# Low parts of X without GpSimd at the two ends of a sequence half, and X loaded once there

## The chip, the cores and the metric

The kernel runs on one core of a Trainium2 chip. A core has five engines that each work through their own instruction queue in order: TensorE (PE: matrix products, with PEld for its weight loads), VectorE (DVE), ScalarE (ACT), GpSimd (POOL) and SyncE (SP, which here only issues DMAs). The metric is the time of one execution on the device in microseconds (us); the median of several runs is given.

## The reference

One decoder block on x (2048 x 1024, fp32) with two token mixers. What the change touches is the first line, the combined input projection; the rest is shown cut:

```python
proj = x @ w_in + b_in                      # (2048, 1024) @ (1024, 9216)
q, k, v, g_attn, u_lru, g_lru, gate_logits = split(proj)
attn = dilated_band_attention(rope(q), rope(k), v) * silu(g_attn)     # three head groups
h    = rg_lru(causal_depthwise_conv(u_lru)) * silu(g_lru)
merged = sigmoid(gA) * (attn @ w_attn_proj) + sigmoid(gB) * (h @ w_lru_proj)
out  = layer_norm(alpha * x + merged @ w_out + b_out)
```

log a in the RG-LRU is -8 r softplus(-lambda), so a softplus of a 1024-vector is needed before the first gate.

## The kernel before

**Numbers.** All matrix products keep fp32 accuracy with operands split into a high and a low part (fp32r): the high part is a rounded copy made by ACT, the low part is the difference (source minus high part), made by DVE or POOL. A product of one 128 x 512 output tile over 512 of the contraction is four K tiles times three matmuls: (w high, x high), (w high, x low), (w low, x high), 12 in all.

**The projection (phase A).** Weight columns are taken in pairs of 128-column blocks: 36 pairs, and for each of the two halves of the sequence one *position* per pair, 72 positions. One position is a 2 x 2 block product: weights A11, A12, A21, A22 (two column blocks, two halves of the contraction) against x blocks B11, B21 (first 512 columns of the half) and B12, B22 (second 512). The first position of each half (s = 0 and s = 36) is computed plainly in eight *ticks*; all others by seven products (Strassen-Winograd, table `MID`, or `EDGE` for the last position of a half): A11·B11, A12·B21, S4·B22, A22·T4, S1·T1, S2·T2, S3·T3. S1 to S4 are sums of weight blocks, T1 to T4 combinations of the x blocks, made once per half. A tick is the time of one product, 12 matmuls; `base[s]` is the tick at which position s starts (0, 8, 15, ..., 253 for s = 36, 261 for s = 37).

**The order.** `manual_schedule` runs each engine in the order of the program text. The loop over ticks writes the product of the tick, then the functions that `at(t, ...)` has put down for it, then the running *chains* (generators that ask for time on engines and are continued when the tick has some left), and then the evacuation of the product's PSUM bank. The product tiles use four PSUM banks in turn (`q`), so the fifth product waits until the first one's bank has been read. An engine that waits holds all that stands behind it.

**Weights.** `load_w` loads a block; for the first half `added` forms S1 and S3 by a DMA that accumulates onto the loaded tile, issued from POOL's queue, `sums` forms S2 and S4 on DVE. `prep_w` makes the high part on ACT and the low part alternately on POOL and DVE; the low parts are kept in DRAM (`wl_scr`) and loaded again for the second half.

**X at the beginning (ticks 0 to 9) and at the change of half (from E0 = base[36] - 7 on).** Each x block has four K tiles of 128 x 512 (256 KB). `load_raw` loads one from DRAM through SP's queue, `hi_lo` makes its two parts; `one_block` does so for a B block, K tiles alternating between DVE and POOL for the low part, and gives the raw tile back. The combinations need the raw data again: `comb_loads` loads all four blocks a second time (tiles `xcB..`), `comb` makes of one K tile T1, T2, T3 and a first step of T4 on DVE, with the copies on ACT and the low parts of T1 and T3 on POOL, and `fourth` makes the parts of T4. T4 shares its place in SBUF with B12, so its copies wait until the plain position is through with B12.

**Around it.** `evacuate` reads a product's bank: product 1 into a copy e by ACT, the others into sums (u, v) and results on DVE; `result` hands a finished tile to a chain (bias, tanh or silu, rotary), and for the merge gates `mg_chain` stores it to `mg_scr` by a DMA on SP. Six small constant operations on DVE and the 25 of softplus stand at the kernel's head and at tick 10, each as one block.

In the traces a name such as xB stands for xB11, xB12, ...; hA and hS are high parts of weights, l low parts, S weight sums, wA and wS raw weights. `hi_lo` is L217 to L221, `tt` L232, so most DVE and POOL operations carry L232 and the parts of X L220 (copy) and L221 (low part); the products are L614.

## Time and profile before

| | |
|---|---|
| time, median of 3 runs | 2311.54 us (2310.54 to 2316.93) |
| profiled execution: time / span | 2308.68 us / 2306.9 us |
| mean granted TensorE clock | 0.983 of full speed |
| DMA: bytes, mean rate | 523.92 MB, 227 GB/s |

The span is the profiled stretch of the program; the time of the same execution lies 1.8 us above it. A page of the profile gives busy time by engine, groups of instructions by source line with the idle time of the engine just before them and what ended it, and DMA issues; the trace behind it can be asked for a timeline of one engine, or for windows with the busy time of every engine in each.

### The profile page before, as it was taken

How to read it: one execution, taken by the hardware profiler on the slowest of the kernel's cores; microseconds unless marked ns; L12 is line 12 of the kernel's file. 1: busy time of each engine (PE TensorE's matmuls, PEld its weight loads, DVE VectorE, ACT ScalarE, POOL GpSimd, SP SyncE). 2: the span in 40 equal slices, each digit the busy share in tenths (PEclk: the TensorE clock that was granted, in tenths of full speed). 3: DMA queues.
4: the chain of work that ended last, by engine and by line, in shares of the span. 5: the costliest groups of instructions: out<-in, count | busy, mean ns of one | idle time of the engine just before them, and what ended most of it. 6: DMA issues, size and time to landing. Idle time of an engine off the chain costs nothing.

```text
span 2306.9 us, 34335 instructions
## 1 busy us (share of the span) xinstructions
PE 2224.7 (96%) x11008; PEld 1871.6 (81%) x11008; DVE 1753.8 (76%) x3192; ACT 1090.9 (47%) x1977; POOL 940.0 (41%) x684
## 2 busy tenths in 40 slices
PE   6999999999999799999999999989999999989998
PEld 4788888888888688888888888879999878768886
DVE  6788888899899767787778878646666568747677
ACT  4346345456455456556566566556666611121100
POOL 5554554555555522222222212357676346612220
PEclk8999999999999899999999999989999999999999
DMA  7897997988988887687786776896986589864431
GB/s 243 233 268 232 277 271 237 276 262 270 283 258 256 274 235 220 191 235 225 221 233 211 227 222 224 252 248 166 246 209 157 166 260 309 265 220 164 155 119 64
DMA packets 332051, 523.92 MB, mean 227 GB/s; under 512 B 97376, under 2 KB 138336, under 8 KB 327264
## 3 DMA queue, kind: packets, MB, share of 16 engines
q1 hardware_dynamic: 303120, 480.63, 67.2%
q0 software_dynamic: 10080, 18.35, 5.0%
q10 hardware_dynamic: 18672, 22.75, 3.2%
q8 instruction: 88, 1.44, 0.3%
q14 instruction: 91, 0.75, 0.1%
HBM read 316.28 MB, written 180.16 MB: 215 GB/s over the span
## 4 chain that ended last, share of the span: by engine, by line
PE 76%; DMA 8%; DVE 6%; issue 5%; POOL 2%; ACT 2%; SPq 1%; ACTq 0%; DVEq 0%; POOLq 0%
PE q L614 55%; PE o L997 4%; PE s L958 3%; PE pt L973 2%; DMA A<-qh_scr 2%; PE yb L1186 2%; PE yb L1187 2%; PE yb L1185 2%; PE z L1279 1%; PE z L1278 1%; PE z L1277 1%; DVE xcB L232 1%; POOL me L1251 1%; DMA xB<-in_xT_dram 1%; PE vtp L367 1%
## 5 line engine op out<-in xcount | busy, mean ns | idle before, releaser
L614 PE MATMUL q<-xT,hS 128*128 128x512 f32 x1680 | 525.2, 394 | 8.7 <-ACT hS L277 6.5
L614 PE MATMUL q<-xT,l 128*128 128x512 f32 x1120 | 439.2, 392 | 2.1 <-DVE l L232 2.1
L614 PE MATMUL q<-xB,hA 128*128 128x512 f32 x1248 | 390.5, 394 | 17.8 <-ACT hA L277 10.3
L614 PEld LDWEIGHTS q<-xT,hS 128*128 128x128 f32 x1680 | 317.5, 190 | 76.5 <-ACT hS L277 7.7
L614 PE MATMUL q<-xB,l 128*128 128x512 f32 x904 | 354.6, 392 | 9.2 <-POOL l L232 9.2
L614 PEld LDWEIGHTS q<-xB,hA 128*128 128x128 f32 x1248 | 236.0, 190 | 68.3 <-ACT hA L277 10.7
L614 PEld LDWEIGHTS q<-xT,l 128*128 128x128 f32 x1120 | 212.0, 189 | 47.8 <-DVE l L232 3.2
L964 ACT ACTIVATE p<-p,osb 128x256 f32<-128x256 f32 (+1 forms) x384 | 156.6, 455 | 115.9 <-DVE osb L962 112.6
L614 PEld LDWEIGHTS q<-xB,l 128*128 128x128 f32 x904 | 171.1, 189 | 46.1 <-POOL l L232 10.0
L232 POOL TENSOR_TENSOR S<-S,wA 128x512 f32<-128x512 f32 x35 | 45.7, 1306 | 386.3 <-DVE S L232 297.8
L962 DVE CUSTOM_DVE_ANT_0 p<-s,mask 128x256 f32<-128x256 f32 (+1 forms) x384 | 125.4, 363 | 101.2 <-PE s L958 64.6
L232 POOL TENSOR_TENSOR sw<-sw,sin 128x512 f32<-128x512 f32 x96 | 159.9, 1685 | 72.0 <-DMA sw<-y 63.4
L614 PE MATMUL q<-xB,hS 128*128 128x512 f32 x560 | 173.7, 391 | 1.1 <-DVE v L232 1.1
L997 PE MATMUL o<-V,ptb 128*128 128x65 f32 x1200 | 165.1, 276 | 9.9 <-ACT ptb L978 6.9
L614 PE MATMUL q<-xT,hA 128*128 128x512 f32 x560 | 173.0, 390 | 0.0
L997 PEld LDWEIGHTS o<-V,ptb 128*128 128x128 f32 x1200 | 152.1, 195 | 21.1 <-ACT ptb L978 17.4
L277 ACT ACTIVATE hA<-wA 128x512 fp32r<-128x512 f32 x218 | 135.4, 623 | 59.2 <-DMA wA<-in_w_in_dram 28.5
L277 ACT ACTIVATE hS<-S 128x512 fp32r<-128x512 f32 x175 | 109.0, 623 | 96.7 <-DVE S L232 55.7
L232 POOL TENSOR_TENSOR l<-wA,hA 128x512 fp32r<-128x512 f32 x74 | 116.1, 1568 | 55.5 <-ACT hA L277 36.5
L958 PE MATMUL s<-B,A 128*128 128x256 f32 (+1 forms) x384 | 117.5, 327 | 6.9 <-POOL B L808 3.6
L1251 POOL TENSOR_TENSOR me<-gA,ybr 128x512 f32<-128x512 f32 x32 | 47.4, 1496 | 188.0 <-DVE gA L1250 183.2
L614 PEld LDWEIGHTS q<-xB,hS 128*128 128x128 f32 x560 | 104.2, 188 | 23.0 <-ACT hS L277 1.2
(196 smaller groups left out, 4967.4 us busy)
## 6 DMA issues: line engine op xcount, KB each, us to landing
wA<-in_w_in_dram SPq DMA_DIRECT2D x253, 256.0 KB, 4.7
wl_scr<-l SPq DMA_DIRECT2D x105, 512.0 KB, 5.0
l<-wl_scr SPq DMA_DIRECT2D x105, 512.0 KB, 4.6
sw<-y SPq DMA_DIRECT2D x384, 64.0 KB, 3.2
wS<-in_w_in_dram SPq DMA_DIRECT2D x70, 256.0 KB, 5.0
wS<-in_w_in_dram POOLq DMA_DIRECT2D x70, 256.0 KB, 7.0
mg_scr<-y SPq DMA_DIRECT2D x59, 256.0 KB, 5.8
o_scr<-osb ACTq DMA_DIRECT2D x48, 264.0 KB, 5.8
```

The source lines that it names most:

```text
L232: eng.tensor_tensor(out=out, in0=in0, in1=in1, op=op)
L277: act.activation(h, r, AF.Copy)
L614: pe.matmul(bank, w[:, ks], x[:, kk, xx], start=(first and i == 0), stop=(last and i == 11))
L958: pe.matmul(s[:, h, (0 if g == 2 and n else lo):256], q, k, start=(i == 0), stop=(i == 1))
L962: dve.tensor_tensor_reduce(out=p[:, h, lo:256], in0=s[:, h, lo:256], in1=mask[:, lo:256], scale=1.0, scalar=3e38, op0=ALU.add, op1=ALU.min ...
L964: act.activation(p[:, h, lo:256], p[:, h, lo:256], AF.Exp, scale=-1.0, bias=mm)
L973: pe.transpose(pt[:, 2 * h + x, :], p[:, h, x * P:(x + 1) * P], ident)
L997: pe.matmul(o[:, n % 2, h * 65:h * 65 + 65], ptb[:, 2 * h + x, :], V[:, kb, vo + h * 65:vo + h * 65 + 65], start=(x == lo // P), stop=(x = ...
L1185: pe.matmul(yb, WL[f][:, 0, k], xx[:, 0], start=(k == 0), stop=False)
L1186: pe.matmul(yb, WL[f][:, 0, k], xx[:, 1], start=False, stop=False)
L1187: pe.matmul(yb, WL[f][:, 1, k], xx[:, 0], start=False, stop=(k == 7))
L1251: pool.tensor_tensor(out=ME[c][:, f], in0=ga, in1=yb, op=ALU.add)
```

## The change

At both places the x tiles are loaded once, as `xcB..` tiles, and kept until the combinations have used them (32 loads of 256 KB fewer). All low parts of X, and those of the weights of positions 0, 1 and 36, are made on DVE. A tick's combinations are three DVE operations per K tile, done in place; the two parts of each T follow in later ticks. The small constants move behind the low parts of B21, and softplus becomes a chain. The first position of seven products in each half takes a new order `FIRST`, in which product 3 comes third and its bank is copied by ACT (p). From three ticks after the start of position 34 until the start of position 38 (two positions after 36), `mg_chain` issues its store from ACT's queue instead of SP's.

```diff
-    MID, EDGE = (1, 6, 7, 5, 2, 4, 3), (1, 2, 6, 7, 4, 5, 3)
+    MID, EDGE, FIRST = (1, 6, 7, 5, 2, 4, 3), (1, 2, 6, 7, 4, 5, 3), (1, 2, 3, 6, 7, 5, 4)
...
-            eng = pool if j % 2 == 0 else dve
+            eng = pool if j % 2 == 0 and s not in (0, 1, len(seq)) else dve
...
+        if base[len(seq) - 2] + 3 <= now["n"] < base[len(seq) + 2]:
+            act.dma_start(mg_scr[i * P:(i + 1) * P, c * CH:(c + 1) * CH], y)
+            yield Ask()
+            give_sent(y)
+            return
...
+        elif order.index(5) > j:
+            Q["p3"] = take(f"p{s}", F32)
+            act.activation(Q["p3"], b, AF.Copy)
...
-            at(t0 - 4, lambda s=s: added(s, "S1", "A22"))
-            at(t0 - 4, lambda s=s: added(s, "S3", "A11"))
-        at(t0 - 1, lambda s=s: sums(s))
+            for n, x in (("S1", "A22"), ("S3", "A11")):
+                at(max(t0 - 4, 2), lambda s=s, n=n, x=x: added(s, n, x))
+        at(max(t0 - 1, 4), lambda s=s: sums(s))
...
     def comb(kk):
-        r11, r12, r21, r22 = (xr["c" + b, kk] for b in ("B11", "B12", "B21", "B22"))
...
+        r11, r12, r22 = (xr["c" + b, kk] for b in ("B11", "B12", "B22"))
         tt(dve, r11, r11, r12, ALU.subtract)
         tt(dve, r12, r22, r12, ALU.subtract)
-        hi_lo("T1", kk, r11, pool)
-        tt(dve, r21, r11, r21, ALU.subtract)
-        hi_lo("T3", kk, r12, pool)
-        tt(dve, r11, r11, r22, ALU.add)
-        hi_lo("T2", kk, r11, dve)
-        tt(dve, r21, r21, r22, ALU.add)
...
+        tt(dve, r22, r11, r22, ALU.add)
+        spend(DVE=2.1)
+
+    def comb4(kk):
+
+        tt(dve, xr["cB21", kk], xr["cB22", kk], xr["cB21", kk], ALU.subtract)
...
-    bring(E0 + 2, "B11", 2, some)
-    bring(E0 + 3, "B21", 2, some)
-    bring(E0 + 6, "B12", 3, some)
-    bring(E0 + 7, "B22", 3, some)
+    for t, b, c in ((2, "B11", 2), (3, "B21", 2), (6, "B12", 3), (7, "B22", 3)):
+        bring(E0 + t, b, c)
     for kk in K4:
-        at(E0 + 6 + kk, lambda kk=kk: comb_loads(2, kk))
-        at(E0 + 9 + kk, lambda kk=kk: comb(kk))
-    at(E0 + 14, lambda: [fourth(kk) for kk in K4])
+        at(E0 + 8 + kk, lambda kk=kk: comb(kk))
+        at(E0 + 9 + kk, lambda kk=kk: comb_part("T2", kk))
+        at(E0 + 9 + kk, lambda kk=kk: comb4(kk))
+    for n, t in (("T3", 13), ("T1", 15), ("T4", 16)):
+        at(E0 + t, lambda n=n: [comb_part(n, kk) for kk in K4])
...
+    at(0, lambda: [one_block("B21", kk) for kk in K4])
+    at(0, consts)
     at(1, lambda: prep_w(0, 2))
...
+    at(1, lambda: [one_block("B12", kk) for kk in K4])
     at(1, lambda: prep_w(0, 3))
...
+    at(2, lambda: [one_block("B22", kk) for kk in K4])
     for kk in K4:
-        at(3 + kk, lambda kk=kk: comb(kk))
-    at(7, lambda: [fourth(kk) for kk in K4])
-    at(10, scales)
+        at(3 + kk // 2, lambda kk=kk: comb(kk))
...
+    for kk in K4:
+        at(4 + kk // 2, lambda kk=kk: comb_part("T2", kk))
+    for n, t in (("T3", 6), ("T1", 7), ("T4", 8)):
+        for kk in K4:
+            if n == "T4":
+                at(t, lambda kk=kk: comb4(kk))
+            at(t, lambda n=n, kk=kk: comb_part(n, kk))
+    at(10, lambda: start_chain(scales()))
```

`comb_part` is `hi_lo` for one K tile of a T, and `keep_raw` is `load_raw` under the name `xcB..`.

**DVE at the beginning, from the end of B22's low parts on.** A name's digits are the block, the position or half and the K tile (xcB1210: block B12, columns 1, K tile 0), and the last number only tells tiles apart. Before:

```order
L232 TENSOR_TENSOR xcB1100_296<-xcB1100_296,xcB1210_298 128x512
L232 TENSOR_TENSOR xcB1210_298<-xcB2210_300,xcB1210_298 128x512
L232 TENSOR_TENSOR xcB2100_302<-xcB1100_296,xcB2100_302 128x512
L232 TENSOR_TENSOR xcB1100_296<-xcB1100_296,xcB2210_300 128x512
L221 TENSOR_TENSOR xT2_406<-xcB1100_296,xT2_406 128x512
L232 TENSOR_TENSOR xcB2100_302<-xcB2100_302,xcB2210_300 128x512
L232 TENSOR_TENSOR S2_1_419<-wS1_1_304,wA11_1_308 128x512
L232 TENSOR_TENSOR S4_1_421<-S2_1_419,wA12_1_341 128x512
L232 TENSOR_TENSOR xcB1101_328<-xcB1101_328,xcB1211_330 128x512
L232 TENSOR_TENSOR xcB1211_330<-xcB2211_332,xcB1211_330 128x512
```

and now, from the same place:

```order
L211 TENSOR_TENSOR xcB1100_214<-xcB1100_214,xcB1210_236 128x512
L211 TENSOR_TENSOR xcB1210_236<-xcB2210_244,xcB1210_236 128x512
L211 TENSOR_TENSOR xcB2210_244<-xcB1100_214,xcB2210_244 128x512
L211 TENSOR_TENSOR xcB1101_216<-xcB1101_216,xcB1211_238 128x512
L211 TENSOR_TENSOR xcB1211_238<-xcB2211_246,xcB1211_238 128x512
L211 TENSOR_TENSOR xcB2211_246<-xcB1101_216,xcB2211_246 128x512
L211 TENSOR_TENSOR xcB1102_218<-xcB1102_218,xcB1212_240 128x512
L211 TENSOR_TENSOR xcB1212_240<-xcB2212_248,xcB1212_240 128x512
L211 TENSOR_TENSOR xcB2212_248<-xcB1102_218,xcB2212_248 128x512
L211 TENSOR_TENSOR xcB1103_220<-xcB1103_220,xcB1213_242 128x512
L211 TENSOR_TENSOR xcB1213_242<-xcB2213_250,xcB1213_242 128x512
```

The low part of T2 and the two steps of T4 stood between the combinations of one K tile; now the combinations of all K tiles follow one another, and all low parts stand behind them.

**ACT around the copies of T4 at the beginning.** hS3_1 and hS1_1 are high parts for position 1, e1 is the copy of its first product's bank, y a result of position 0. Before:

```order
L277 ACTIVATE hS3_1_510<-wS3_1_306 128x512
L220 ACTIVATE xT4_527<-xcB2100_302 128x512
L220 ACTIVATE xT4_527<-xcB2101_334 128x512
L220 ACTIVATE xT4_527<-xcB2102_373 128x512
L220 ACTIVATE xT4_527<-xcB2103_403 128x512
L277 ACTIVATE hS1_1_536<-wS1_1_304 128x512
L393 ACTIVATE y64_1_544<-q6_0_486,bh_178 128x512
L277 ACTIVATE hA12_1_559<-wA12_1_341 128x512
L637 ACTIVATE e1_568<-q0_1_546 128x512
L277 ACTIVATE hA22_1_583<-wA22_1_339 128x512
```

and now:

```order
L372 ACTIVATE y64_1_495<-q6_0_439,bh_178 128x512
L256 ACTIVATE hS3_1_510<-wS3_1_298 128x512
L199 ACTIVATE xT4_519<-xcB2100_224 128x512
L199 ACTIVATE xT4_519<-xcB2101_226 128x512
L199 ACTIVATE xT4_519<-xcB2102_228 128x512
L199 ACTIVATE xT4_519<-xcB2103_230 128x512
L618 ACTIVATE e1_532<-q0_1_497 128x512
L256 ACTIVATE hS1_1_547<-wS1_1_296 128x512
L256 ACTIVATE hA22_1_566<-wA22_1_330 128x512
L637 ACTIVATE p1_574<-q2_1_553 128x512
L256 ACTIVATE hA11_2_589<-wA11_2_481 128x512
```

e1 stood behind the T4 copies before as well. What the T4 copies wait for has changed: each now follows a DVE operation (`comb4`) of its own K tile, which on DVE alternates with the low parts of T4. p1 is the new copy of the third product's bank.

**ACT at the change of half, up to the first high part of position 37.** Before:

```order
L220 ACTIVATE xT1_7431<-xcB1121_7378 128x512
L220 ACTIVATE xT3_7433<-xcB1231_7380 128x512
L220 ACTIVATE xT2_7432<-xcB1121_7378 128x512
L393 ACTIVATE y64_2_7479<-q2_36_7414,bh_178 128x512
L220 ACTIVATE xT1_7431<-xcB1122_7402 128x512
L220 ACTIVATE xT3_7433<-xcB1232_7404 128x512
L220 ACTIVATE xT2_7432<-xcB1122_7402 128x512
L277 ACTIVATE hA11_37_7527<-wA11_37_7427 128x512
L220 ACTIVATE xT1_7431<-xcB1123_7445 128x512
L220 ACTIVATE xT3_7433<-xcB1233_7447 128x512
L220 ACTIVATE xT2_7432<-xcB1123_7445 128x512
L393 ACTIVATE y56_3_7540<-q4_36_7481,bh_178 128x512
```

and now:

```order
L378 DMA mg_scr_72<-y56_2_7359 128x512
L199 ACTIVATE xT2_7379<-xcB2230_7249 128x512
L199 ACTIVATE xT2_7379<-xcB2231_7251 128x512
L372 ACTIVATE y64_2_7404<-q2_36_7362,bh_178 128x512
L378 DMA mg_scr_72<-y64_2_7404 128x512
L199 ACTIVATE xT2_7379<-xcB2232_7253 128x512
L256 ACTIVATE hA11_37_7447<-wA11_37_7375 128x512
L199 ACTIVATE xT2_7379<-xcB2233_7255 128x512
L372 ACTIVATE y56_3_7452<-q4_36_7407,bh_178 128x512
L378 DMA mg_scr_72<-y56_3_7452 128x512
L256 ACTIVATE hA12_37_7468<-wA12_37_7377 128x512
```

Ahead of hA11_37 there stand three copies of T2 now, one for each K tile, where there were three T copies for each, and stores to mg_scr stand among them.

More of the change, by code (lines that the diff above doesn't have):

```diff
@@ L549, in hybrid_block_kernel @@
         for p, (kind, f0, f1) in enumerate(seq):
[L550 removed]
+            plan.append((h, ((f0, kind), (f1, kind)), None if p == 0 else EDGE if p == len(seq) - 1 else FIRST if p == 1 else MID, p, kind))
     NQ = len(plan)
@@ L695, in hybrid_block_kernel, with keep_raw, one_block @@
             at(base[s] - 12, lambda i=i: start_chain(lru(i, 1, None)))
-    def some(kk):
-        return pool if kk % 2 else dve
-    def one_block(b, c, kk, eng):
+    def keep_raw(b, c, kk):
+        load_raw(b, c, kk, "c")
+    def one_block(b, kk):
         if kk == 0:
             new_block(b)
-        hi_lo(b, kk, xr[b, kk], eng)
-        drop_raw(b, kk)
-        if eng is dve:
-            spend(ACT=.66, DVE=.72)
-        else:
-            spend(ACT=.66, POOL=1.4)
-    def comb_loads(c0, kk):
-        for b, c in (("B11", c0), ("B12", c0 + 1), ("B22", c0 + 1), ("B21", c0)):
-            load_raw(b, c, kk, "c")
+        hi_lo(b, kk, xr["c" + b, kk])
+        spend(ACT=.66, DVE=.72)
@@ L725, in comb @@
-        hi_lo("T2", kk, r11, dve)
-        tt(dve, r21, r21, r22, ALU.add)
-        for b in ("B11", "B12", "B22"):
-            drop_raw("c" + b, kk)
-        spend(ACT=2.0, DVE=4.3, POOL=2.8)
-    def fourth(kk):
-        if kk == 0:
-            new_block("T4")
-        hi_lo("T4", kk, xr["cB21", kk], some(kk))
-        drop_raw("cB21", kk)
-        spend(ACT=.66, DVE=.36, POOL=.7)
+        tt(dve, r22, r11, r22, ALU.add)
+        spend(DVE=2.1)
+    def comb4(kk):
+        tt(dve, xr["cB21", kk], xr["cB22", kk], xr["cB21", kk], ALU.subtract)
+        drop_raw("cB22", kk)
+        spend(DVE=.7)
```

90 lines of the change are left out of this document (46 added, 44 removed).

## The prediction

> **What bounds the kernel now.** I read the head of the page first, then idle time by line in the two stretches that the change touches, then the rows there.
>
> ```profile
> span 2306.9 us, 34335 instructions
> PE 2224.7 (96%) x11008; PEld 1871.6 (81%) x11008; DVE 1753.8 (76%) x3192; ACT 1090.9 (47%) x1977; POOL 940.0 (41%) x684
> ```
>
> TensorE is busy for 96% of the span, so another engine matters only where TensorE waits for it. Windows (us, then busy time and count of each engine; PEclk is the granted clock) show where that is at the beginning:
>
> ```profile
> 0.00:20.00 20.00, 8.36 (x26) 5.87 (x26) 11.91 (x22) 13.44 (x22) 8.46 (x14) 0.95 0.94 332
> 20.00:40.00 20.00, 15.36 (x60) 12.57 (x61) 9.62 (x13) 3.98 (x7) 13.38 (x11) 0.79 0.86 289
> 40.00:60.00 20.00, 13.30 (x40) 8.84 (x39) 15.52 (x17) 8.90 (x16) 10.01 (x8) 0.72 0.23 79
> 60.00:80.00 20.00, 17.27 (x63) 13.33 (x62) 18.06 (x39) 7.00 (x14) 9.44 (x10) 0.85 0.75 209
> 80.00:100.00 20.00, 20.00 (x90) 16.54 (x89) 12.18 (x16) 6.05 (x11) 11.18 (x10) 1.00 0.91 255
> ```
>
> After 80 us TensorE is full and its clock is 1.00: 90 matmuls in 20 us. Its groups by line (busy, mean ns, then idle time before them and who ended it), 0 to 100 us and then 690 to 830 us:
>
> ```profile
> L614 PE MATMUL q<-xB,hA 128*128 128x512 f32 x103 | 34.9, 419 | 7.5 <-ACT xB L220 5.7 <-DVE xB L221 1.8
> L614 PE MATMUL q<-xB,l 128*128 128x512 f32 x59 | 24.5, 415 | 9.2 <-POOL l L232 9.2
> L614 PE MATMUL q<-xT,hS 128*128 128x512 f32 x48 | 19.7, 497 | 6.1 <-ACT hS L277 4.0 <-ACT xT L220 2.1
> L614 PE MATMUL q<-xT,l 128*128 128x512 f32 x32 | 15.0, 469 | 2.1 <-DVE l L232 2.1
> L614 PE MATMUL q<-xB,hA 128*128 128x512 f32 x147 | 47.2, 403 | 10.3 <-ACT hA L277 10.3
> L614 PE MATMUL q<-xT,hS 128*128 128x512 f32 x120 | 38.3, 401 | 2.5 <-ACT hS L277 2.5
> ```
>
> The timeline of TensorE (start, duration, ..., idle before and releaser) gives the landmarks:
>
> ```profile
> 5.68 0.80 PE L614 MATMUL q<-xB,hA 128*128 128x512 f32 x1 [5.68 <-ACT xB L220]
> 24.64 0.79 PE L614 MATMUL q<-xB,l 128*128 128x512 f32 x1 [8.81 <-POOL l L232]
> 45.52 0.39 PE L614 MATMUL q<-xB,l 128*128 128x512 f32 x1
> 78.90 0.62 PE L614 MATMUL q<-xB,hA 128*128 128x512 f32 x2
> ...
> 776.90 0.39 PE L614 MATMUL q<-xB,l 128*128 128x512 f32 x1
> 787.55 1.22 PE L614 MATMUL q<-xB,hA 128*128 128x512 f32 x2 [10.27 <-ACT hA L277]
> 795.57 0.72 PE L614 MATMUL q<-xT,hS 128*128 128x512 f32 x2 [2.54 <-ACT hS L277]
> 813.63 0.62 PE L614 MATMUL q<-xB,hA 128*128 128x512 f32 x2
> ...
> 814.31 0.62 PE L614 MATMUL q<-xB,hA 128*128 128x512 f32 x2
> ```
>
> Three matmuls pass between the last two rows: 0.68 us, 0.227 each, so a tick of 12 costs 2.72. From the first matmul (5.68) to position 2 (78.90) 73.2 us pass; 15 ticks are 40.8. The **beginning loses 32.4 us**. From the end of position 36 (776.90 + 0.39 = 777.3) to position 38 (813.63) 36.3 us pass; 7 ticks are 19.0. The **half change loses 17.3 us**. These 49.7 us are all that the change can win.
>
> **The change part by part: beginning.** The prices come from these rows (DVE, ACT, POOL, and one group of DMA issues with its median us to landing):
>
> ```profile
> 6.17 0.17 DVE L427 TENSOR_SCALAR lrn<-lr 128x32 f32<-128x32 f32 x1
> 20.37 2.01 DVE L232 TENSOR_TENSOR xcB<-xcB,xcB 128x512 f32<-128x512 f32 x3
> 30.78 1.77 DVE L232 TENSOR_TENSOR xcB<-xcB,xcB 128x512 f32<-128x512 f32 x1 [8.39 <-POOL xT L221]
> 33.24 0.69 DVE L221 TENSOR_TENSOR xT<-xcB,xT 128x512 fp32r<-128x512 f32 x1 [0.70 <-ACT xT L220]
> 62.50 3.09 DVE L232 TENSOR_TENSOR l<-wS,hS 128x512 fp32r<-128x512 f32 x1
> 73.82 0.17 DVE L849 TENSOR_SCALAR sp2n<-sp 128x8 f32<-128x8 f32 x1
> 77.22 0.68 DVE L232 TENSOR_TENSOR l<-S,hS 128x512 fp32r<-128x512 f32 x1
> 77.82 0.68 DVE L232 TENSOR_TENSOR y<-q,e 128x512 f32<-128x512 f32 x1
> ...
> 7.71 0.63 ACT L220 ACTIVATE xB<-xB 128x512 fp32r<-128x512 f32 x1 [0.76 <-DMA xB<-in_xT_dram]
> 15.99 4.25 ACT L220 ACTIVATE xB<-xB 128x512 fp32r<-128x512 f32 x8
> ...
> 21.39 1.91 POOL L250 DMA_DIRECT2D wS<-in_w_in_dram  x2 [8.05 <-DMA wS<-in_w_in_dram]
> ...
> wS<-in_w_in_dram POOLq DMA_DIRECT2D x70, 256.0 KB, 7.0
> ```
>
> A DVE operation costs 0.60 (77.22 to 77.82), a chain of three dependent ones about 2.05; beside a busy POOL the same low part took 3.09. An ACT copy costs 0.53 (4.25 / 8). POOL is where the 8.81 us arise: its queue holds two accumulating DMAs that wait 8.05 us for the weights they add to, and the low parts of A21 and of half of B12 and B22 stand behind them. It also holds DVE for 8.39 us, since the fourth combination overwrites what POOL's low part still reads. The change takes every one of these low parts off POOL, so both waits go, and DVE runs at the undisturbed price. DVE then carries them alone, and I walk its queue in the new order.
>
> Loads: the fifth 256 KB load has landed at 7.7 (row 7.71), and at 250 to 400 GB/s of the windows, say 384, one takes 0.68. The 20 loads of position 0 stand first as before: B12 lands by 15.2, B22 by 18.0, and the five weights of position 1, ahead of which no second copies of X stand now, by 21.3.
>
> - First product: the 1.8 us <-DVE xB go, a low part behind the six constant operations; its 24 matmuls end near 13. The constants, about 1 us at 0.17 each (row 6.17), move into the time in which DVE waits for the next loads, at 12; without that cover they cost that 1 us.
> - Low parts of A21, B12, A22, B22 on DVE end near 20, ahead of the product that needs them at 22. About 1 us of small stalls (A21 and A22, each behind its load and one ACT copy) stay. 5.7 + 8 x 2.72 + 1.8 for the cold start and the first loads + 1.0: position 0 ends at **30.3** (before, 45.52 + 0.39 = 45.9).
> - Combinations: 12 DVE operations, 4 x 2.05 = 8.2, until 28.1. Then the two weight sums and A11's low part, until 30.0: position 1 starts at 30.3 without a gap. The T2, T3, T1 low parts and the weight low parts follow at 0.60 and stay 1 to 2 us ahead of TensorE; the last ends at 39.6. Four products end at 41.2.
> - Now a **new wait**. The fifth product takes the PSUM bank of the first, which ACT empties by the copy e. In ACT's new order e stands behind the four T4 copies, and each of these waits for a DVE combination that in DVE's queue alternates with the low part of the tile before it: combination 0.60, copy 0.70 (the wait of row 33.24), low part 0.60, about 1.9 to 2.0 a tile. Four of them from 39.0 to 39.6 end the last copy at 46.9 and e at 47.5. TensorE stands 6.3 us. Behind e in ACT's queue are the copies of S1 and A22 and that of the third product's bank, 0.53 each; products 6 and 7 want them 5 us later, so they add nothing.
> - It then restarts at half clock. After 787.55 the next 12 matmuls end at 795.57 - 2.54 = 793.0, 5.5 instead of 2.7. This stall is shorter than that of 10.27, so of 0 to 2.8 I take 2.2. Three products more, and position 2 starts at 47.5 + 8.2 + 2.2 = **57.9**.
>
> Before 78.9, after 57.9: **21.0 us won**. Without the wait it would be 30.3 + 19.0 = 49.4, that is 29.5. With DVE 3 us later all along it is 18. The Trainium skill ("TensorE: Matmul & The Clock Gate", section "What's actually happening") gives a half-rate clock for about one window of 3.4 us of sustained work after an idle one; that would price the restart at 1.7, an estimate, and make the sum 21.5. The row of 787.55 shows more lost than that, because a further wait comes before the clock is back.
>
> The softplus chain, 25 operations at 0.17 to 0.20 (row 73.82), was one block of some 5 us or more; now it is spread over ticks 10 to 30, and a tick leaves DVE about 1 us free (12.18 busy of 20 in 80 to 100). I cost it at nothing; all of it uncovered would be 5. FIRST puts product 3 early and adds one ACT copy (0.6): inside the same walk.
>
> **Half change.** What TensorE waits for, 10.27 us, is one ACT copy (hA) behind copies of combinations:
>
> ```profile
> 761.07 2.49 ACT L220 ACTIVATE xB<-xB 128x512 fp32r<-128x512 f32 x4 [1.77 <-DMA xB<-in_xT_dram]
> ...
> 786.35 0.63 ACT L220 ACTIVATE xT<-xcB 128x512 fp32r<-128x512 f32 x1 [2.71 <-DVE xcB L232]
> 786.88 0.61 ACT L277 ACTIVATE hA<-wA 128x512 fp32r<-128x512 f32 x1
> ...
> 780.62 5.70 DVE L232 TENSOR_TENSOR xcB<-xcB,xcB 128x512 f32<-128x512 f32 x4
> ...
> mg_scr<-y SPq DMA_DIRECT2D x14, 256.0 KB, 6.4
> ```
>
> By DVE's rows there a K tile took 8 us (four operations 5.70 beside POOL), four K tiles over 30. In the new order only T2 is made inside the K tile: 2.05 + 0.70 + 0.60 + 0.60 = 3.9 us, so from the end of B22's low parts (764.2: their ACT copies, behind a load, end at 761.07 + 2.49 = 763.6 as before) the K tiles end at 768.1, 772.0, 776.7 (two weight sums in part beside the copy) and 780.5. The copy hA of position 37 stands behind the third T2 copy and ends at 775.4, needed at 777.3. The next weight copies end at 780.7 (needed 780.0) and 783.5 (needed 782.7); T3, T1 and T4 low parts end at 783.6, 787.4, 790.6, each before its product. Left are about 1 us of stalls: **16.3 us won**. Bounds: 17.3 if none is left; if DVE's operations cost 1.2 to 1.4 each wherever POOL works (5.70 / 4), 16 of them 8 us later and 8 won.
>
> Fifteen stores to mg_scr move from SP to ACT in these ticks. An issue costs ACT at most what one cost POOL (row 21.39, 1.91 for two), 14 us over some 50. ACT is half idle there (8.64 of 20 in 760 to 780):
>
> ```profile
> 760.00:780.00 20.00, 17.28 (x77) 13.97 (x75) 14.01 (x16) 8.64 (x14) 9.49 (x7) 0.98 1.06 356
> ```
>
> I cost it at nothing beyond the walk. The DMA share is 1.06, and 16 loads of 256 KB less in each stretch (11 us of it at 0.68) relieve it.
>
> **Sum.** 21.0 + 16.3 = 37.3. The profiled execution took 2308.68 (span 2306.9, the rest around it): 2271.4. The median of the runs shown, 2311.54, lies 2.9 above the profiled one: **2274**.
>
> **The rivals.**
> - *No bank wait.* If the T4 chain runs ahead (e by 41.2), the beginning wins 29.5: about 2265. For it: DVE may be some us ahead by then. Against: the order itself, e behind four copies that wait in turn. 0.17.
> - *DVE is now the bound at the half change.* With POOL's rotary products still beside it, the K tiles take 6 us, and the waits come back in part: 8 us less won, about 2282. For it: 780.62 and a slack of under 2 us; against: POOL has no low parts of X then. 0.22.
> - *Loads bind the beginning.* The weight sum of position 1 needs an accumulating DMA that is issued after a load at 18.7 and takes about 7 us: 26.6, needed at 28.1. If it comes 4 us later, everything behind it in DVE's queue does: about 2278. 0.07.
> - *Slower.* ACT issues 15 stores, in a queue in which weight and X copies stand. If an issue holds ACT until an earlier transfer of its queue has landed, each costs up to 6.4 (row of mg_scr): 96 us. Six of them that reach TensorE (38 us) use up the gain; eight would give 2274 + 51 = 2325. Against: SP issues the same stores today among its loads, and these keep the DMA engines full. 0.03. The Trainium skill ("DMA: Bandwidth & Descriptors", section "Issuing engines are not separate DMA queues") says that moving a DMA to another engine saves issue time only, since all share the same engines. By that rule the move by itself wins nothing; the sum holds nothing for it. No row of before tests it here.
> - *The change doesn't do what it says.* The order shows POOL without a low part until position 2, so this holds only if DVE pays as much as POOL did: 2300 or more, 0.01.
>
> **How the numbers follow.** Forecast as walked 0.50 (2270 to 2278); the rivals 0.17, 0.22, 0.07, 0.03, 0.01. 2262 (all 49.7 won) to 2288 (half change wins little) holds about nine in ten, and the two unknown prices, DVE beside POOL and the restart, don't let me cut it further. About 0.3% (7 us) is what a measurement tells from no change; faster 0.95, same 0.02, slower 0.03.
>
> **What would show it.** Position 0's last matmul near 30, no idle time <-POOL l before 60 us; one idle time of about 6 us <-ACT e before the fifth product of position 1, at 41 to 48; position 2 at 58. At the half change no idle time over 2 us and hA ended before TensorE needs it. I am wrong if DVE's rows beside POOL stay near 1.4 there, if a load or the accumulating DMA ends a wait at the beginning, or if ACT shows idle time behind an issue.

## The result, and the profile after

| | before | after |
|---|---|---|
| time, median | 2311.97 us (4 runs, 2310.54 to 2316.93) | 2287.77 us (4 runs, 2284.91 to 2295.28) |
| ratio, 95% interval | | 0.989 [0.9868, 0.9913] |
| profiled execution: time / span | 2308.68 / 2306.9 us | 2284.91 / 2282.8 us |

The changed kernel is faster by 24.2 us; 37.3 were forecast. The time lies 13.8 us above the likeliest value, outside the 2270 to 2278 us that carried half of the chance, and 0.2 us inside the end of the whole range (2288). The head of the page and the windows of the beginning, of the changed kernel (in a window's row: its bounds and length; busy time and count of PE, PEld, DVE, ACT and POOL; granted clock, DMA share, GB/s):

```profile
span 2282.8 us, 34216 instructions
PE 2219.8 (97%) x11008; PEld 1870.6 (82%) x11008; DVE 1743.3 (76%) x3228; ACT 1094.8 (48%) x1979; POOL 872.3 (38%) x640
```

```profile
0.00:20.00 20.00, 14.23 (x49) 10.81 (x50) 13.83 (x32) 13.91 (x23) 2.39 (x11) 1.00 0.93 325
20.00:40.00 20.00, 20.00 (x90) 16.55 (x89) 19.69 (x33) 11.24 (x20) 2.71 (x4) 1.00 0.85 228
40.00:60.00 20.00, 14.01 (x53) 11.06 (x52) 14.45 (x21) 10.03 (x17) 5.93 (x5) 0.83 0.52 154
```

TensorE is now full from 20 to 40 us (20.00 busy at clock 1.00, where it had 15.36 at 0.79) and has one gap, in the third window. Its groups from 0 to 100 us name what is left:

```profile
L595 PE MATMUL q<-xB,hA 128*128 128x512 f32 x120 | 39.3, 409 | 5.8 <-ACT xB L199 5.8
L595 PE MATMUL q<-xB,l 128*128 128x512 f32 x72 | 29.1, 404 | 0.0
L595 PE MATMUL q<-xT,hS 128*128 128x512 f32 x76 | 25.2, 415 | 6.0 <-ACT e L618 6.0
```

The 9.2 us behind POOL's low parts are gone; 5.8 is the start of the program, and 6.0 is the predicted wait for the copy e. The timeline of TensorE (start, duration, ..., idle time before and releaser) holds the last matmul of position 0 (30.45), the starts of positions 1, 2, 36 and 38 (30.67, 58.15, 740.68, 787.16) and the longer waits between them:

```profile
30.45 0.39 PE L595 MATMUL q<-xB,l 128*128 128x512 f32 x1
30.67 0.61 PE L595 MATMUL q<-xB,hA 128*128 128x512 f32 x2
...
47.70 1.22 PE L595 MATMUL q<-xT,hS 128*128 128x512 f32 x2 [5.99 <-ACT e L618]
...
58.15 0.62 PE L595 MATMUL q<-xB,hA 128*128 128x512 f32 x2
...
315.04 0.70 PE L595 MATMUL q<-xT,hA 128*128 128x512 f32 x2 [1.30 <-ACT hi L320]
...
340.47 0.70 PE L595 MATMUL q<-xB,hS 128*128 128x512 f32 x2 [2.63 <-DVE v L211]
...
740.68 0.62 PE L595 MATMUL q<-xB,hA 128*128 128x512 f32 x2
...
769.13 1.22 PE L595 MATMUL q<-xB,hA 128*128 128x512 f32 x2 [3.75 <-ACT hA L256]
...
787.16 0.62 PE L595 MATMUL q<-xB,hA 128*128 128x512 f32 x2
```

From these landmarks the span can be cut into four parts. Positions 36 and 37 are 15 ticks, 40.8 us when nothing waits; what lies above that is called lost.

| us | before | after | won | forecast |
|---|---|---|---|---|
| start of position 2 | 78.90 | 58.15 | 20.75 | 21.0 |
| position 2 to 36 | 676.46 | 682.53 | -6.07 | 0 |
| position 36 to 38 | 58.27 | 46.48 | 11.79 | 16.3 |
| position 38 to the end | 1493.27 | 1495.64 | -2.37 | 0 |

The beginning came out as walked, to 0.2 us. Of the 13.2 us that are missing (37.3 less 24.1), 6.1 were lost in a stretch that the change does not touch, 4.5 at the half change, and 2.4 behind position 38. The last part runs the same instructions in all kernels below, and there it took between 1488.99 and 1501.27 us, without any order by what was changed; the four runs of the changed kernel alone lie 10.4 us apart. So it is read as the spread from one execution to the next.

### The profile page after: what moved, and what is told of

It reads as the page before. It is cut to its first block, busy times and chain, and to the rows that moved or that the text cites. A ratio compares the mean times of both kernels' runs of the same rounds, so it can differ in the third digit from the quotient of the medians.

```text
span 2282.8 us, 34216 instructions
## 1 busy us (share of the span) xinstructions
PE 2219.8 (97%) x11008; PEld 1870.6 (82%) x11008; DVE 1743.3 (76%) x3228; ACT 1094.8 (48%) x1979; POOL 872.3 (38%) x640
## 4 chain that ended last, share of the span: by engine, by line
PE 75%; DMA 7%; DVE 7%; issue 6%; ACT 2%; POOL 2%; SPq 1%; ACTq 0%; DVEq 0%; POOLq 0%
PE q L595 55%; PE o L1005 4%; PE s L966 3%; PE pt L981 2%; DMA A<-qh_scr 2%; PE z L1287 1%; PE z L1286 1%; PE z L1285 1%; PE yb L1194 1%; PE yb L1195 1%; PE yb L1193 1%; POOL me L1259 1%; PE vtp L346 1%; ACT p L972 1%; PE g L467 1%
## 5 line engine op out<-in xcount | busy, mean ns | idle before, releaser
L211 POOL TENSOR_TENSOR l<-wA,hA 128x512 fp32r<-128x512 f32 x68 | 106.3, 1563 | 81.6 <-ACT hA L256 64.9
L595 PEld LDWEIGHTS q<-xT,hA 128*128 128x128 f32 x560 | 104.8, 188 | 24.4 <-ACT hi L320 1.7
L595 PEld LDWEIGHTS q<-xB,hS 128*128 128x128 f32 x560 | 104.1, 188 | 24.7 <-issue 3.8
```

The lines of the kernel that those rows point to most:

```text
L211: eng.tensor_tensor(out=out, in0=in0, in1=in1, op=op)
L595: pe.matmul(bank, w[:, ks], x[:, kk, xx], start=(first and i == 0), stop=(last and i == 11))
```

## The experiments

All kernels start from the changed one unless said otherwise. The table holds what the texts below refer to; "lost" is the part of positions 36 to 38 above 40.8 us, and the ratio is to the kernel before, timed on the same chip. The expectations count the middle to the end of position 36, 22 us further (698.4 and 704.5 there are 676.5 and 682.5 here), and the half change whole, not only what is lost (46.5 there is 5.7 here).

| kernel | position 2 starts | 2 to 36 | lost at 36 to 38 | 38 to end | median us (runs) | ratio [95%] |
|---|---|---|---|---|---|---|
| before | 78.90 | 676.46 | 17.5 | 1493.27 | 2311.97 (4) | |
| after | 58.15 | 682.53 | 5.7 | 1495.64 | 2287.77 (4) | 0.989 [0.9868, 0.9913] |
| begin_only | 57.76 | 687.59 | 16.8 | 1492.89 | 2297.53 (4) | 0.9925 [0.9899, 0.9951] |
| half_only | 79.31 | 679.36 | 7.0 | 1489.74 | 2302.24 (8) | 0.9957 [0.9941, 0.9974] |
| debt | 58.30 | 678.43 | 5.5 | 1493.59 | 2277.60 (4) | 0.9843 [0.9818, 0.9868] |
| t4_flat | 51.73 | 683.52 | 6.6 | 1501.27 | 2279.94 (4) | 0.9856 [0.9828, 0.9885] |
| hA12_early | 57.45 | 685.37 | 5.3 | 1493.68 | 2281.63 (4) | 0.986 [0.9838, 0.9882] |
| h_early | 58.10 | 685.62 | 4.0 | 1494.03 | 2285.44 (4) | 0.9873 [0.9847, 0.9899] |
| stores_sp | 57.70 | 684.78 | 2.6 | 1496.14 | 2284.02 (4) | 0.9869 [0.9845, 0.9893] |
| pool_lows | 60.97 | 677.05 | 6.8 | 1496.25 | 2282.13 (4) | 0.9859 [0.9837, 0.9881] |
| best1 | 49.85 | 678.51 | 2.5 | 1488.99 | 2266.50 (4) | 0.9815 [0.9795, 0.9835] |
| best2 | 49.35 | 680.87 | 0.0 | 1490.58 | 2269.05 (5) | 0.9818 [0.9801, 0.9835] |

Single steps of a few us are close to the intervals of the ratios (about 0.25% either way, 6 us), so what is said of single steps goes by the stretches of one profile for each kernel. The times confirm the change itself and best1 and best2; they do not tell the single steps apart (kernels from different chips are compared by their ratios).

### One half of the change alone: begin_only and half_only

begin_only keeps the beginning and takes back the half change (loads, `comb`, `fourth`, the product order, stores on SP, POOL's low parts of position 36); the diff is shown cut:

```diff
-            eng = pool if j % 2 == 0 and s not in (0, 1, len(seq)) else dve
+            eng = pool if j % 2 == 0 and s not in (0, 1) else dve
-        if base[len(seq) - 2] + 3 <= now["n"] < base[len(seq) + 2]:
-            act.dma_start(mg_scr[i * P:(i + 1) * P, c * CH:(c + 1) * CH], y)
...
-        at(E0 + 8 + kk, lambda kk=kk: comb(kk))
+        at(E0 + 6 + kk, lambda kk=kk: comb_loads(2, kk))
+        at(E0 + 9 + kk, lambda kk=kk: comb_b(kk))
...
```

half_only is the kernel before with the new half change and nothing else.

> The changed beginning with the old half change (X loaded twice there, low parts shared with POOL, order MID, stores on SP). Theory: the beginning's gain is its own, and the 6.1 us that the changed kernel loses between positions 2 and 36 (704.5 us instead of 698.4) come with it, because the planner's DVE budget is overdrawn by 19.7 us at tick 8. Then position 2 starts at 58.2, the middle takes 704.5, the half change loses 17 us again, and the profiled time is near 2294. Rival: the middle's loss belongs to the half change's edits or to that one execution: middle 698.5, time near 2288.

> The old beginning with the changed half change. Theory: the wait of 3.75 us before the second product of position 37 is made by the half change's own order (ACT copy behind the fourth T2 copy): the middle takes 698.4 as before, the half change loses 5 to 6 us of the old 17.3, time near 2297. Rival: that wait comes from chains pushed late by the beginning: then the half change loses under 2 us, time near 2293.

The timeline of TensorE in begin_only:

```profile
315.44 0.70 PE L590 MATMUL q<-xT,hA 128*128 128x512 f32 x2 [1.75 <-ACT hi L320]
...
340.85 0.70 PE L590 MATMUL q<-xB,hS 128*128 128x512 f32 x2 [2.64 <-DVE v L211]
...
776.81 1.22 PE L590 MATMUL q<-xB,hA 128*128 128x512 f32 x2 [9.55 <-ACT hA L256]
784.82 0.73 PE L590 MATMUL q<-xT,hS 128*128 128x512 f32 x2 [2.52 <-ACT hS L256]
```

The half change is as before the change (16.8 lost, the same two waits), and the waits at 315 and 340 us are there: they come from the beginning. The middle took 5.1 us more than expected, for reasons given under debt. half_only has neither of them (679.36 from position 2 to 36) and loses 7.0 at the half change, with 0.94 and 3.82 us <-ACT hA: the wait that is left there is the half change's own. The two ratios multiply to 0.988, the whole change gave 0.989: within the intervals the halves add up.

### What the beginning does to positions 2 to 36: debt

The loop over ticks keeps an account of DVE's time: each tick pays in, each operation spends, and a chain is continued only while something is left. At the beginning all low parts of X are now charged to DVE, and the account goes into the red; the chains that are then held back come up in other ticks. This kernel wipes out that debt and changes nothing else:

```diff
+        if T == 16:
+            left["DVE"] = LEN
```

> The changed kernel with one line more: the planner's DVE budget is set back to one tick's worth at tick 16, so that chains start as in the kernel before. Theory of the overdrawn budget: the idle times of 2.6 and 1.3 us near 315 and 340 us go, the middle takes 698.4 to 700 instead of 704.5, and the time is 5 to 6 us below that of the changed kernel, 2279 to 2282. Rival (DVE really has too much work after the beginning, or chance): chains that start earlier collide with it, idle times appear between 60 and 120 us, and the middle stays at 704 or gets longer.

The groups of TensorE from 300 to 360 us, first of the changed kernel, then of debt:

```profile
L595 PE MATMUL q<-xT,hA 128*128 128x512 f32 x16 | 5.1, 401 | 1.3 <-ACT hi L320 1.3
L595 PE MATMUL q<-xB,hS 128*128 128x512 f32 x16 | 5.1, 401 | 2.6 <-DVE v L211 2.6
```

```profile
L595 PE MATMUL q<-xT,hA 128*128 128x512 f32 x24 | 7.5, 393 | 0.0
L595 PE MATMUL q<-xB,hS 128*128 128x512 f32 x20 | 6.2, 390 | 0.0
```

Both waits are gone, and the stretch takes 678.43 instead of 682.53. What they were is seen on DVE in the changed kernel: three steps of a chain (the short convolution, L442) stand ahead of the sum v that empties a PSUM bank, and TensorE, which needs that bank, starts at 340.47, just after v ends (339.65 + 0.68 = 340.33).

```profile
336.44 3.29 DVE L442 SCALAR_TENSOR_TENSOR v<-ub,lrn,v 128x512 f32<-128x512 f32 x3
339.65 0.68 DVE L211 TENSOR_TENSOR v<-u,q 128x512 f32<-128x512 f32 x1
```

Over the twelve profiles the two waits sort the stretch without overlap: the six kernels without them (before, half_only, debt, pool_lows, best1, best2) took 676.5 to 680.9 us, the six with them 682.5 to 687.6. In four of these six (begin_only, hA12_early, h_early, stores_sp) the granted clock falls to half for 3.4 us behind the wait near 340; they took 684.8 to 687.6, the two others (after, t4_flat) 682.5 and 683.5. So the state of that account, and through it the order of the chains, is the cause of this loss. The waits in the changed kernel add up to some 4.5 us of the 6.1; for the rest no wait is named. The two profiled spans differ by 6.2 us, of which 4.1 lie in this stretch and 2.1 behind position 38; the median, 2277.60, lies a little below what was expected. Another wait of 0.4 to 1.5 us near 590 us (609 in half_only; <-ACT hi) comes and goes among the kernels, and debt has it with 1.03 where the changed kernel does not; it is not tied to anything that was changed.

### The wait for e: t4_flat

The four combinations of T4 are written ahead of the four copies, so that DVE's queue no longer alternates between them and the low parts:

```diff
+    for kk in K4:
+        at(8, lambda kk=kk: comb4(kk))
...
-            if n == "T4":
-                at(t, lambda kk=kk: comb4(kk))
```

> The changed kernel with the four T4 combinations on DVE in a row ahead of the T4 copies and low parts (they alternated), all else the same. Theory: ACT's copy e stands late because each T4 copy waits for a DVE operation that follows the low part before it; without that, e ends near 42 instead of 47.65, the wait before the fifth product of position 1 falls from 6.0 us to about 1, position 2 starts at 51 to 52 instead of 58.2. Rival: the wait only moves (to the copy p, or to DVE's sums for the sixth and seventh product): position 2 at 55 or later.

The chain that this breaks up, in the changed kernel, on DVE and then on ACT:

```profile
39.85 0.68 DVE L211 TENSOR_TENSOR xcB<-xcB,xcB 128x512 f32<-128x512 f32 x1
41.23 0.69 DVE L200 TENSOR_TENSOR xT<-xcB,xT 128x512 fp32r<-128x512 f32 x1 [0.70 <-ACT xT L199]
41.84 0.68 DVE L211 TENSOR_TENSOR xcB<-xcB,xcB 128x512 f32<-128x512 f32 x1
43.22 0.69 DVE L200 TENSOR_TENSOR xT<-xcB,xT 128x512 fp32r<-128x512 f32 x1 [0.70 <-ACT xT L199]
```

```profile
46.54 0.63 ACT L199 ACTIVATE xT<-xcB 128x512 fp32r<-128x512 f32 x1 [1.36 <-DVE xcB L211]
47.07 0.58 ACT L618 ACTIVATE e<-q 128x512 f32<-128x512 f32 x1
```

Each engine waits for the other once per K tile: a turn takes 1.99 us (43.22 less 41.23), and four of them stand ahead of e. In t4_flat TensorE shows:

```profile
43.44 0.73 PE L595 MATMUL q<-xT,hS 128*128 128x512 f32 x2 [1.83 <-ACT e L618]
```

1.83 us is left of 5.99, the clock stays up, and position 2 starts 6.4 us earlier. The chain of the two queues is shown to be the wait, with 0.8 more left than expected.

### The wait at the half change: hA12_early and h_early

After the change TensorE waits 3.75 us at 769.13 for hA12, the weight of the second product of position 37; the first product runs without a wait. hA12_early writes the preparation of that weight a tick earlier, ahead of the fourth T2 copy; h_early does so for the second, third and fourth weights.

```diff
-            at(t0 + j, lambda s=s, j=j: prep_w(s, j))
+            at(t0 + j - ({1: 1} if s == len(seq) + 1 else {}).get(j, 0), lambda s=s, j=j: prep_w(s, j))
```

(h_early has `{1: 1, 2: 1, 3: 1}`.)

> The changed kernel with one weight copy of position 37 (hA12) a tick earlier, so that it stands ahead of the fourth T2 copy on ACT. Theory: the wait of 3.75 us is ACT's queue order alone; but the next copy of its kind (hS4, for the third product) stands behind the four T3 copies and ended at 771.7 in the changed kernel, 3.8 us after TensorE would want it at 767.9. So the wait moves to the third product, nearly whole, and the half change (start of position 36 to start of position 38) falls by less than 1.5 us from 46.5. Rival: the DVE queue (combinations slowed by POOL) is the limit and the copy's place is nothing: the wait stays before the second product.

> The same with three weight copies (hA12, hS4, hS2) a tick earlier, ahead of the T copies of that tick. Theory of ACT's queue order: only hS4 is still about 1 us late (its weight sum is made on POOL), so 46.5 us become 42 to 43 (15 ticks at full clock are 40.8), and the time falls by about 4 us. Rival (DVE is the limit): T2 and T3 low parts are late next, 45 or more.

TensorE in hA12_early:

```profile
773.59 0.73 PE L595 MATMUL q<-xB,hS 128*128 128x512 f32 x2 [3.17 <-ACT hS L256]
```

The wait moved one product on, from hA to hS, and 0.4 us were won, as expected: the place of one copy alone is not the bound. In h_early four waits of 1.09, 0.17, 0.57 and 0.73 us take its place, and 4.0 are lost in all, between what the two theories gave. That run alone does not decide between them.

### The stores on ACT: stores_sp

The branch of `mg_chain` that issues the store from ACT is taken out; SP issues all of them, as before.

```diff
-        if base[len(seq) - 2] + 3 <= now["n"] < base[len(seq) + 2]:
-            act.dma_start(mg_scr[i * P:(i + 1) * P, c * CH:(c + 1) * CH], y)
-            yield Ask()
-            give_sent(y)
-            return
```

> The changed kernel with the mg_scr stores issued from SP again. My forecast costed the move at nothing. Theory: a store costs ACT 0.33 us of issue and 0.4 behind it, and one stands right ahead of hA12; from SP the wait of 3.75 us is 3.0 to 3.4 and the half change 45.5 to 46. Rival: on SP the stores, which wait for ACT's results, hold up the loads behind them, and a wait for a load appears at the half change: 47 us or more.

ACT in the changed kernel, and then TensorE in stores_sp:

```profile
750.33 0.33 ACTq L378 DMA_DIRECT2D mg_scr<-y  x1
750.70 0.72 ACT L372 ACTIVATE y<-y,bh 128x512 f32<-128x512 f32 x1 [0.40 <-DVE xB L200]
...
767.37 0.67 ACT L372 ACTIVATE y<-q,bh 128x512 f32<-128x512 f32 x1
768.07 0.33 ACTq L378 DMA_DIRECT2D mg_scr<-y  x1
768.44 0.63 ACT L256 ACTIVATE hA<-wA 128x512 fp32r<-128x512 f32 x1 [0.40 <-ACT y L372]
```

```profile
769.36 0.74 PE L590 MATMUL q<-xB,hA 128*128 128x512 f32 x2 [2.24 <-ACT hA L256]
```

From the end of y (767.37 + 0.67 = 768.04) to the start of hA 0.40 us pass: that is what one store takes out of ACT's queue. One stands ahead of hA12 and three (the first at 750.33) right ahead of the first T2 copy. Without them the wait is 2.24 instead of 3.75, and the half change loses 2.6 instead of 5.7, more than was expected of the edit.

Not all of these 3.1 us are the price of the stores. From the start of the first combination to the end of hA12 the changed kernel takes 18.75 us (750.32 to 769.07), the four others with the stores on ACT and hA12 in its place 18.75 to 19.09, and stores_sp 17.81: the stores cost 0.94 us in ACT's queue, and that they cost nothing, as the prediction had it, is refuted. Another 0.62 of the shorter wait comes from combinations that began earlier (9.02 us after the start of position 36, not 9.64). They stand behind X's last loads, and this start varies from 9.40 to 10.90 where ACT issues the stores and is 9.84 in best1, where SP does; so it is not shown to be the stores' doing. The remaining 1.6 us were saved because the clock did not go down behind the shorter wait, and the last section shows that this was partly luck. The times do not confirm the gain (ratios 0.9869 and 0.989, each with about 0.0023 either way). The Trainium skill ("DMA: Bandwidth & Descriptors", section "Issuing engines are not separate DMA queues") says that moving a DMA to another engine saves only the time in which the engine's sequencer issues it, usually small beside the transfer. The trace agrees that an issue is short, 0.40 us, and shows the other side of it: in a queue on which TensorE waits, a few of them cost 0.94 us.

### Where POOL's price lay: pool_lows

Half of the low parts of X and of the weights of position 0 go back to POOL. Loading once, the order of the combinations and everything else stay.

```diff
-            eng = pool if j % 2 == 0 and s not in (0, 1, len(seq)) else dve
+            eng = pool if j % 2 == 0 and s not in (1, len(seq)) else dve
...
-        hi_lo(b, kk, xr["c" + b, kk])
+        hi_lo(b, kk, xr["c" + b, kk], pool if kk % 2 and now["n"] < 10 else dve)
```

> The changed kernel with half of the low parts of B11, B21, B12, B22 and of the weights A11, A21 of position 0 on POOL again, and the accumulating DMAs behind them (before they stood ahead). It separates two reasons for the gain at the beginning. Theory of the prediction: POOL's own price (1.3 to 1.9 us a low part, and DVE slowed beside it) matters too, so the third product of position 1 starts 2 to 5 us later than the 36.1 of the changed kernel and position 2 at 60 or later. Rival: all came from the accumulating DMAs that blocked POOL's queue for 8 us: the third product starts within 1 us of 36.1, position 2 within 1 us of 58.2.

TensorE, DVE and POOL in pool_lows:

```profile
20.37 0.50 PE L595 MATMUL q<-xB,l 128*128 128x512 f32 x1 [2.19 <-DVE l L211]
```

```profile
18.57 1.75 DVE L211 TENSOR_TENSOR l<-wA,hA 128x512 fp32r<-128x512 f32 x1
...
22.54 8.49 DVE L211 TENSOR_TENSOR xcB<-xcB,xcB 128x512 f32<-128x512 f32 x12
```

```profile
15.07 6.39 POOL L200 TENSOR_TENSOR xB<-xcB,xB 128x512 fp32r<-128x512 f32 x4
21.41 1.91 POOL L229 DMA_DIRECT2D wS<-in_w_in_dram  x2
```

POOL's accumulating DMAs stand behind its low parts here, so no low part waits for them; and yet TensorE waits 2.19 at 20.37, and the combinations start at 22.54 instead of 20.07. A DVE low part takes 1.7 us beside POOL (18.57 until 20.24), and 0.60 alone. So POOL's work itself, and what it does to DVE, has a price, and the wait behind the accumulating DMAs was not the whole of what the change removed. Position 1 starts 4.6 us later than in the changed kernel (35.25 against 30.67) and position 2 2.8 us later. What the wait behind the accumulating DMAs cost by itself was not measured apart. The Trainium skill ("SBUF — State Buffer", section "Who interferes with whom") states that a DVE instruction with two inputs in SBUF contends with a GpSimd instruction that reads SBUF; these rows show it, at nearly three times the duration.

A surprise beside it: the middle took 677.05, without the waits at 315 and 340. The time charged for X to DVE's account is the same here as in the changed kernel, since the charge was left as it is; only two weights, 1.86 us of charge, are no longer charged to DVE. Here v starts at 333.41 and the three steps of the convolution behind it, at 334.01. So the size of the overdraft alone does not decide; which chain step comes to stand ahead of which evacuation does.

### All of it together: best1 and best2

best1 joins t4_flat (the copies of T4 a tick later still), debt, h_early and stores_sp. best2 is best1 with the combinations of the next K tile written ahead of the low part of T2 at the half change, as t4_flat does it at the beginning:

```diff
     for kk in K4:
         at(E0 + 8 + kk, lambda kk=kk: comb(kk))
+    for kk in K4:
         at(E0 + 9 + kk, lambda kk=kk: comb_part("T2", kk))
         at(E0 + 9 + kk, lambda kk=kk: comb4(kk))
```

> The changed kernel with four edits together: the T4 combinations in a row and the T4 copies a tick later, so that the copy e stands ahead of them; the DVE budget set back at tick 16; the three weight copies of position 37 a tick earlier; the mg_scr stores on SP. If the three causes are separate and add up: no wait for e, position 2 at 50 to 51; the middle (position 2 to 36) 676.5 to 678.5; the half change 42 to 43 us; with a rest of 1493 to 1497 the time is 2264 to 2268. If they are one slack that is used only once, 2272 or more.

> The same with the combinations of the next K tile ahead of the low part of T2 at the half change, so that DVE need not stand 0.70 us for each of four ACT copies. If DVE's chain of 4.1 to 4.6 us a K tile is what is left there, the third product's weight copy and the T parts come 2 to 3 us earlier and the half change falls to 41 to 42 us (15 ticks are 40.8), the time 1 to 2 us below the other. If loads or POOL's weight sum bind there, no difference.

DVE at the half change, first of the changed kernel, then of best2:

```profile
750.32 2.14 DVE L211 TENSOR_TENSOR xcB<-xcB,xcB 128x512 f32<-128x512 f32 x3
753.58 0.69 DVE L200 TENSOR_TENSOR xT<-xcB,xT 128x512 fp32r<-128x512 f32 x1 [1.12 <-ACT xT L199]
...
757.70 0.69 DVE L200 TENSOR_TENSOR xT<-xcB,xT 128x512 fp32r<-128x512 f32 x1 [0.70 <-ACT xT L199]
758.30 2.74 DVE L211 TENSOR_TENSOR xcB<-xcB,xcB 128x512 f32<-128x512 f32 x4
...
762.90 3.91 DVE L211 TENSOR_TENSOR xcB<-xcB,xcB 128x512 f32<-128x512 f32 x4
```

```profile
738.36 4.26 DVE L211 TENSOR_TENSOR xcB<-xcB,xcB 128x512 f32<-128x512 f32 x6
742.54 0.68 DVE L200 TENSOR_TENSOR xT<-xcB,xT 128x512 fp32r<-128x512 f32 x1
```

In best2 six combinations run through, the copy of T2 is ready when its low part is due, and neither the 1.12 nor the 0.70 us appears. From the first combination to the last low part of T2 14.87 us pass, in best1 16.75. Positions 36 to 38 take 40.80: nothing is lost there any more. But in this execution X's last loads also landed early, and the combinations began 1.70 us earlier than in best1 (8.14 against 9.84 after the start of position 36); so the last 2.5 us are not shown to be the new order's alone. Both kernels beat the kernel before by 1.8%, and by the ratios the changed one by about 17 us. In the profiles 5 to 6.6 us of the lead over the changed kernel lie behind position 38 and are not their doing. best1's half change, 43.25, came just above the 42 to 43 expected, best2's below its 41 to 42. Between the two the times decide nothing (2262.60 to 2273.94 and 2262.42 to 2271.22).

## Why the prediction was right, and where it was wrong

**The time: inside the range by luck.** The range ended at 2288 for the case that the half change wins little. That did not happen: it won 11.8 of 16.3 us. What brought the time to that end was a loss in the middle, which no term and no rival of the prediction held, and the spread behind position 38.

**The beginning: right, step by step.** Position 0's last matmul starts at 30.45 (forecast: ends at 30.3), e ends at 47.07 + 0.58 = 47.65 (47.5), TensorE stands 5.99 (6.3), and from the restart to position 2 10.45 us pass, 2.29 more than three ticks (2.2). The 2.2 was a choice out of 0 to 2.8, and its closeness is partly chance: behind the same wait of 5.8 to 6.0 us the six kernels that have it lost 1.9 to 2.7. The 2.8 us lost after the stall of 10.27 were put down to a further wait, and that was a misreading: the clock was at half until 792.89, and the further wait began after that, at 793.0. No wait <-POOL is left, DVE's twelve combinations cost 8.30 (8.2). t4_flat shows that the named cause of the wait, the two queues that alternate, is the right one. The rivals without a bank wait and with a wait on loads fall: no wait there ends with a DMA. Whether loading X once won anything by itself was not tried apart; pool_lows shows only that POOL's part is some of it. Nor was the softplus chain, costed at nothing, tried alone.

**The middle: a term was missing.** The sum took everything between the two ends as unchanged. But the operations that were moved to DVE are also charged to it in the planner's account, and this account decides in which tick the chains run, 100 ticks and more behind the change. That stretch took 6.1 us more, and debt won 4.1 of them back. By the order alone this could have been seen ahead: in the changed kernel three steps of the convolution stand between the weight sums and v, in the kernel before they do not.

**The half change: right in kind, 4.5 us too much.** The long wait was taken away as foreseen (10.27 and 2.54 became one of 3.75), and the next one to be late was one that the walk had as late by a little, the second weight copy, by 0.7 us. Counted from the start of position 36, that copy was to end at 25.3 and ended at 28.4 (768.44 + 0.63 less 740.68), with TensorE ready at 24.7. Three terms make up 2.9 of these 3.05 us. The **stores on ACT** were costed at nothing beyond the walk and took 0.94. The **start of the combinations**, behind X's last loads, was put at 8.84 (764.2 less 755.36) and came at 9.64, 0.80 later. And four operations of the **last K tile** took 3.91 instead of 2.74, 1.17 more, beside POOL's weight sum: the low parts of T2 follow one another at 4.12, 4.59 and 5.21 us, where the walk had 3.9, 4.7 and 3.8.

```profile
762.51 1.62 POOL L211 TENSOR_TENSOR S<-S,wA 128x512 f32<-128x512 f32 x1 [30.11 <-DMA wA<-in_w_in_dram]
```

The rival "DVE is now the bound" thus held in part, at one K tile of four and not at 6 us. That POOL's sum is to blame is read from rows; it was not taken away by itself. In best2, where it falls on three other operations of DVE, those take 3.18 us, and three take 2.14 without it (750.32 above), which speaks for it. To 3.75 us of waiting the restart at half clock added 1.9, which the forecast had at the beginning only.

**Slower through the stores** fell at the price it named (an issue held until a transfer has landed): an issue takes 0.40 us. But idle time of ACT behind an issue, which the prediction named as a sign of being wrong, is there, and it reached TensorE.

**The end** lost 2.4 us in the profiled execution, in code that was not changed; by the spread of 12 us among the kernels above this says nothing of the change.

## What to carry to other kernels

When two in-order queues hand work to each other once per tile, write all of the first engine's steps ahead of the second's (t4_flat, best2): here the turnaround, not the work, was the price. A planner that charges engines for work must be looked at beyond the edit, since a moved charge shifts what runs hundreds of microseconds later; here wiping it out won 4.1 us in the profile, more than moving the weight copies did. And a DMA issue is not free on an engine that hands its results to the critical path, even at 0.40 us.

## What the runs showed of the hardware

What a short wait costs depends not only on its length, but on where it falls. In all twelve profiles the stretches of half clock begin and end on a fixed grid of 3.41 us (to within 3 ns, one grid for each execution). From 14 to 830 us every step of that grid in which TensorE stood idle for 1.91 us or more was followed by a step at half clock; after a step at full clock with 1.60 us or less idle, the clock stayed up. Two waits of nearly the same length, 2.19 us at 20.37 in pool_lows and 2.24 us at 769.36 in stores_sp, show it. The windows are steps of the grid, two of pool_lows and then one of stores_sp:

```profile
17.68:21.09 3.41, 1.22 (x6) 0.71 (x5) 3.41 (x3) 1.22 (x3) 3.41 (x3) 1.00 0.94 349
21.09:24.50 3.41, 3.41 (x10) 2.64 (x9) 3.34 (x5) 0.04 (x1) 2.23 (x3) 0.50 0.39 52
```

```profile
768.24:771.66 3.42, 2.30 (x10) 1.89 (x11) 3.09 (x5) 3.42 (x7) 0.00 (x0) 1.00 0.60 159
```

The first wait lies whole in one step (TensorE busy 1.22 of 3.41), and the next step runs at clock 0.50. The second is cut in two: 1.12 us idle in this step and 1.12 in the one before, and the step behind it is at 1.00. So stores_sp lost only 0.34 us beyond its wait until position 38, where waits of 3.17 (hA12_early), 3.56 (debt) and 3.75 us (after) lost 2.1, 1.9 and 1.9 more, and a wait of 2.24 us that fell otherwise could have cost more. The same holds for the wait of 2.63 us near 340: after kept its clock behind it (1.17 and 1.46 idle in two steps), h_early did not (2.26 in one).

By the same grid the slow stretch need not begin with the restart. In debt:

```profile
764.93 0.73 PE L595 MATMUL q<-xB,hA 128*128 128x512 f32 x2 [3.56 <-ACT hA L256]
...
766.54 1.05 PE L595 MATMUL q<-xB,hA 128*128 128x512 f32 x2
...
770.07 0.62 PE L595 MATMUL q<-xB,hS 128*128 128x512 f32 x2
```

The first pair behind the wait still takes 0.73, a pair 1.6 us later 1.05, and one 5 us after the restart 0.62 again.
